# Seven block products instead of eight in the last block of three projections

## The chip, the core and the metric

The kernel runs on one core of one Trainium2 chip. The metric is device time in microseconds (us) from launch to end, as the median of several runs. One execution was also profiled: it gives the start and the length of every instruction on the engines. These are TensorE (PE; its weight loads are listed apart as PEld), VectorE (DVE), ScalarE (ACT), GpSimd (POOL) and the queue of SyncE (SP) that issues DMAs.

## The reference

The kernel computes one layer of a streaming encoder on 2048 tokens of width 1024, in float32:

```
u = rms_norm(h, g_mix_pre);  z = u @ w_in
ya = swa_with_sinks(...z...);  yh = hgrn2(...z...)          # two groups of heads
y = concatenate([ya, yh]) @ w_out                           # the out projection
h = h + rms_norm(y, g_mix_post)
u = rms_norm(h, g_x_pre);  m = rms_norm(mem, g_mem)
s = (u @ wq) . (m @ wk);  p = softmax(s);  y = (p . (m @ wv)) @ wo   # 4 heads, 256 memory tokens
h = h + rms_norm(y, g_x_post)
u = rms_norm(h, g_ffn_pre)
y = (silu(u @ w_gate) * (u @ w_up)) @ w_down
h = h + rms_norm(y, g_ffn_post)
```

The kernel folds wq with the memory's keys into one 1024 x 1024 matrix, and the memory's values with wo into another. So the cross attention is two more products of the same form: tokens by "qk" gives the scores, softmax of the scores by "vo" gives the output.

## The kernel before

A float32 factor is split into a high part that TensorE takes directly (fp32r) and the remainder, low. A product of two such factors is three matmuls: high by high, high by low, low by high (L1122, L1123 and L1124 in `products`).

**Jobs and blocks.** Behind the attention, the work is a list of jobs (`jobs`, L1418): the out projection, the scores ("qk"), the values ("vo"), two halves of the gate and up projections of the feed-forward part, and three parts of the down projection. A job holds one resident operand, called T, of 2 x 2 quarters (each up to four slices of 128 rows, 512 columns), and streams the other, called S, in blocks. The out projection, the scores and the values have eight blocks each, of 256 tokens. A block multiplies a 2 x 2 split of S with the 2 x 2 split of T.

**Two kinds of block.** A block of kind "s" (`seven`, L1126) does Winograd's form of Strassen's scheme: seven products of quarters instead of eight. It takes sums and differences of the quarters: `combine` makes four for S on DVE (L1097), and those for T are made beforehand in DRAM (`combined`). Three intermediate products are copied out of PSUM by ACT (L1137) and added by DVE when a result is taken out (L1498 for the out projection and the values, L1557 for the scores). A block of kind "p" (`eight`, `plain`) does the plain eight products: four quarters of S, no sums, and the results leave PSUM by a copy on ACT alone (L1500), or directly into the softmax. Its products come in an order of its own, and of T it needs the four plain quarters, numbered 1, 2, 8 and 3; a block of kind "s" needs 1, 5, 6, 3, 7, 2 and 4.

**Making operands.** Every S quarter is split by `split2` (L982): the high part on ACT (L985) or POOL (L987), then the low part on DVE (L988), 128 x 512 each. Every T operand comes in two halves of 128 x 1024: a DMA into a row tile, the high part on ACT, the low part on DVE, the same lines. T operands live in seven slots. A slot becomes free with the last step that uses its operand; `half` (L1262) then issues the load of one half of the next operand in order of need, and `split` issues the splitting of a half that was loaded.

**What sets the order.** `phases` (L1210) walks through the steps: after each step (one product in a block of kind "s", two in one of kind "p") it makes the S quarters of two steps ahead, gives each follow-up piece of work of earlier blocks (`after`) a turn, and calls `split` and `half`: once per step in a block of kind "s", twice in one of kind "p". These lines hold for the last block of a job if it is of kind "s" (and `fresh` for the block behind it):

```
change = kind == "s" and i == len(bl) - 1
...
if change or kind == "s" and fresh:
    split(g)
    if change and q in (0, 3, 6):
        half(g, self.row_tile)
```

So such a block splits up to two halves per step, and loads a second one in three of its seven steps. The follow-up work of a block is RMS norms, residual adds, the softmax's scaling, transposes by TensorE (L1381) and stores: L1529 and L1530 for the out projection, L1571 and L1573 for the scores, L1617, L1608 and L1604 for the values, where two blocks also prepare sums of tokens (`token_sums`, L1409 to L1413). A planner of the framework, which estimates times, then fixes the final order of the instructions on every engine; engines run their own queues in that order and wait on each other's semaphores.

In `jobs`, `kinds(blocks, n, last)` gives the first n blocks kind "p", the last block kind `last` (default "p") and the others "s". Before the change, the out projection has kind "p" in its first and its last block, and the scores and the values in their last; the feed-forward jobs have "s" throughout.

Of the kernel before, what the change touches and what calls it, by code (L numbers as in the profile page):

```python
# [29 lines left out]
NT = T // P  # L30
# [18 lines left out]
class Layer:  # L49
# [1121 lines left out]
    def plain(self, S, T, nk, out, keep, kind):  # L1171
# [36 lines left out]
        yield  # L1208

    def phases(self, jobs, first, prologue=None):  # L1210

        steps = [(n, i, p) for n, job in enumerate(jobs) for i, b in enumerate(job[2])
                 for p in self.STEPS[b[0]]]
        takes = [c for job in jobs for b in job[2] for c in self.TAKES[b[0]]]
# [200 lines left out]
    def jobs(self):  # L1418
        I = self.I

        def weights(src, r0, nk):
            return lambda t, i, j, k0, n: self.load(
                t, src[r0 + (i * nk + k0) * P:r0 + (i * nk + k0 + n) * P, j * 512:(j + 1) * 512]
                .rearrange("(k p) d -> p k d", p=P))

        def ffn_u(b):
            return lambda t, i, j, k0, n: self.load(
                t, self.u_d[4 * i + k0:4 * i + k0 + n, :, b * TB + j * 512:b * TB + (j + 1) * 512]
                .rearrange("k p t -> p k t"))

        def kinds(blocks, n=0, last="p"):
            return [("p" if i < n else last if i == len(blocks) - 1 else "s",) + b for i, b in enumerate(blocks)]

        def sums(name, src, nk, other=None):
            return self.sums(name, src, nk, self.extra_tile, other or self.gain_tile)

        def in_turn(*what):
            return lambda: itertools.chain.from_iterable(w() for w in what)

        qk, vo = weights(self.qk_d, 0, 4), weights(self.vo_d, 0, 4)  # L1440
        down = [(weights(I["w_down"], f0 * P, nk), f0, nk) for f0, nk in ((0, 3), (6, 4), (14, 4))]
        qk_s, vo_s = sums("qk_s", qk, 4, self.row_tile), sums("vo_s", vo, 4)
        u_s = sums("u_s", ffn_u(1), 4)
        self.u0_s = self.tc.dram_tile([4, P, 4 * 512], F32, name="u0_s")
        d_s = [sums(f"d_s{c}", src, nk) for c, (src, _, nk) in enumerate(down)]
        jobs = [(self.w_out, 4, kinds([self.mixed_block(n) for n in range(0, NT, 2)], 1), self.out_sums, {1: [qk_s[1]]}),
                (qk, 4, kinds([self.score_block(n) for n in range(0, NT, 2)]), qk_s[0], {1: [vo_s[1]]}),
                (vo, 4, kinds([self.value_block(n) for n in range(0, NT, 2)]), vo_s[0], {})]
        for b in range(NB):
            beside = {2: [in_turn(*(d[1] for d in d_s))]} if b else {4: [u_s[1]]}  # L1450
            jobs.append((ffn_u(b), 4, kinds([blk for f in range(0, NFF, 2) for blk in self.hidden_blocks(b, f)], 0, "s"),
                         u_s[0] if b else self.u0_s, beside))
        for c, (src, f0, nk) in enumerate(down):
            jobs.append((src, nk, kinds([self.down_block(c, f0, nk, n) for n in range(0, NT, 2)], 0, "s"), d_s[c][0], {}))

        return jobs
# [308 lines left out]
```

## Time and profile before

| | us |
|---|---|
| median of 3 runs | 2574.08 |
| lowest and highest | 2572.68, 2574.33 |
| profiled execution, its time | 2572.97 |
| profiled execution, its span from first to last instruction | 2571.3 |
| TensorE busy | 2535.4 |
| VectorE busy | 1764.8 |
| ScalarE busy | 1263.9 |
| GpSimd busy | 425.4 |

Groups of instructions are listed by line, engine, operation and tiles (written <- read), with their count, busy time and mean length in ns, then the engine's idle time before them with what ended it. In a timeline a row has start and length in us, the engine, and in brackets the engine's idle time ahead of it. A table of stretches gives for each stretch its length, the busy time of each engine with the instructions in parentheses, TensorE's granted clock, and the share of the DMA engines. The out projection, the scores and the values run from about 785 us to 1300 us of the span.

### The profile page before, as it was taken

How to read it: one execution, taken by the hardware profiler on the slowest of the kernel's cores; microseconds unless marked ns; L12 is line 12 of the kernel's file. 1: busy time of each engine (PE TensorE's matmuls, PEld its weight loads, DVE VectorE, ACT ScalarE, POOL GpSimd, SP SyncE). 2: the span in 40 equal slices, each digit the busy share in tenths (PEclk: the TensorE clock that was granted, in tenths of full speed). 3: DMA queues.
4: the chain of work that ended last, by engine and by line, in shares of the span. 5: the costliest groups of instructions: out<-in, count | busy, mean ns of one | idle time of the engine just before them, and what ended most of it. 6: DMA issues, size and time to landing. Idle time of an engine off the chain costs nothing.

```text
span 2571.3 us, 34876 instructions
## 1 busy us (share of the span) xinstructions
PE 2535.4 (99%) x12326; PEld 2124.0 (83%) x12326; DVE 1764.8 (69%) x2791; ACT 1263.9 (49%) x2643; POOL 425.4 (17%) x612
## 2 busy tenths in 40 slices
PE   9999999999999999999999999999999999999998
PEld 8888888878987888888778888888888888888886
DVE  7785588887556778788885655576666557574766
ACT  5563466555555565565563333344333335443543
POOL 4231334321312322212310000000000000000022
PEclk9999999999999999999999999999999999999999
DMA  5445755765887896665973622253555425464776
GB/s 189 148 164 170 205 162 163 228 198 160 262 282 276 294 310 209 221 218 198 341 244 117 205 91 74 82 205 117 186 197 196 156 94 182 165 195 106 226 178 152
DMA packets 357295, 486.36 MB, mean 189 GB/s; under 512 B 20352, under 2 KB 248704, under 8 KB 357120
## 3 DMA queue, kind: packets, MB, share of 16 engines
q1 hardware_dynamic: 351072, 462.11, 54.6%
q0 software_dynamic: 6048, 22.02, 4.9%
q8 instruction: 97, 1.59, 0.3%
q14 instruction: 78, 0.64, 0.1%
HBM read 317.34 MB, written 166.72 MB: 188 GB/s over the span
## 4 chain that ended last, share of the span: by engine, by line
PE 82%; DMA 6%; DVE 6%; ACT 2%; issue 2%; POOL 1%; SPq 1%; DVEq 0%; POOLq 0%; ACTq 0%
PE psm L1122 22%; PE psm L1124 22%; PE psm L1123 22%; PE psg L157 2%; PE psg L156 2%; PE psg L158 2%; PE pss L1381 1%; DMA x<-in_w_out_dram 1%; DVE S L988 1%; DMA y_d<-sg 1%; DMA u_d<-row 1%; DVE T L988 0%; SPq L75 0%; DMA qk_s<-extra 0%; DVE S L808 0%
## 5 line engine op out<-in xcount | busy, mean ns | idle before, releaser
L1123 PE MATMUL psm<-T,S 128*128 128x512 f32 x2680 | 1042.9, 390 | 1.4 <-DVE T L988 1.4
L1122 PE MATMUL psm<-T,S 128*128 128x512 f32 x2680 | 1035.2, 391 | 4.9 <-ACT part L1137 3.4
L1124 PE MATMUL psm<-T,S 128*128 128x512 f32 x2680 | 1030.5, 390 | 4.9 <-DVE S L988 4.9
L1122 PEld LDWEIGHTS psm<-T,S 128*128 128x128 f32 x2680 | 503.0, 188 | 113.3 <-ACT part L1137 6.0
L1124 PEld LDWEIGHTS psm<-T,S 128*128 128x128 f32 x2680 | 503.1, 188 | 111.4 <-DVE S L988 7.0
L1123 PEld LDWEIGHTS psm<-T,S 128*128 128x128 f32 x2680 | 503.2, 188 | 106.4 <-DVE T L988 3.8
L985 ACT ACTIVATE S<-sum 128x512 fp32r<-128x512 f32 (+1 forms) x330 | 198.6, 619 | 364.1 <-PE psm L1124 260.9
L988 DVE TENSOR_TENSOR S<-sraw,S 128x512 fp32r<-128x512 f32 (+1 forms) x315 | 214.6, 689 | 229.8 <-ACT S L985 216.4
L988 DVE TENSOR_TENSOR S<-sum,S 128x512 fp32r<-128x512 f32 (+1 forms) x388 | 259.1, 677 | 47.1 <-ACT S L985 32.6
L1137 ACT ACTIVATE part<-psm 128x512 f32<-128x512 f32 x285 | 168.9, 596 | 244.9 <-PE psm L1124 223.6
L985 ACT ACTIVATE S<-sraw 128x512 fp32r<-128x512 f32 (+1 forms) x268 | 165.2, 617 | 110.0 <-PE psm L1124 99.4
L1509 POOL DMA_DIRECT2D y_d<-row x16 | 14.0, 877 | 1077.4 <-DVE row L1695 1026.6
L988 DVE TENSOR_TENSOR T<-row,T 128x1024 fp32r<-128x1024 f32 (+1 forms) x112 | 131.8, 1189 | 35.9 <-ACT T L985 34.1
L157 PE MATMUL psg<-u,whi 128*128 128x512 f32 x320 | 127.8, 399 | 0.0
L158 PE MATMUL psg<-u,wlo 128*128 128x512 f32 x320 | 127.1, 397 | 0.0
L156 PE MATMUL psg<-u,whi 128*128 128x512 f32 x320 | 127.1, 397 | 0.0
L1476 ACT ACTIVATE junk<-row 128x512 f32<-128x512 f32 x160 | 99.7, 625 | 45.7 <-DVE row L1498 27.2
L985 ACT ACTIVATE T<-row 128x1024 fp32r<-128x1024 f32 (+1 forms) x112 | 113.6, 1032 | 8.6 <-DMA row<-d_s 4.3
L987 POOL TENSOR_SCALAR S<-sum 128x512 fp32r<-128x512 f32 x58 | 49.4, 851 | 300.1 <-PE psm L1124 240.9
L1646 DVE TENSOR_TENSOR row<-psm,part 128x512 f32<-128x512 f32 x66 | 43.7, 688 | 68.3 <-PE psm L1124 68.2
L1655 DVE TENSOR_TENSOR part<-psm,part 128x512 f32<-128x512 f32 x66 | 43.8, 688 | 60.2 <-PE psm L1124 60.0
L1695 DVE TENSOR_TENSOR row<-psm,part 128x512 f32<-128x512 f32 x72 | 49.1, 688 | 49.5 <-PE psm L1124 49.4
(364 smaller groups left out, 3715.6 us busy)
## 6 DMA issues: line engine op xcount, KB each, us to landing
sraw<-in_w_gate_dram SPq DMA_DIRECT2D x44, 512.0 KB, 3.6
sraw<-in_w_up_dram SPq DMA_DIRECT2D x44, 512.0 KB, 3.7
hid_d<-row SPq DMA_DIRECT2D x44, 512.0 KB, 2.7
sraw<-hid_d SPq DMA_DIRECT2D x32, 512.0 KB, 4.1
sraw<-in_w_in_dram SPq DMA_DIRECT2D x44, 256.0 KB, 3.6
z_d<-pair SPq DMA_DIRECT2D x20, 512.0 KB, 3.0
raw<-in_w_in_dram SPq DMA_DIRECT2D x20, 512.0 KB, 4.6
z_d<-z SPq DMA_DIRECT2D x20, 512.0 KB, 4.0
```

The costliest lines, as they stand in the source:

```text
L156: nc.tensor.matmul(ps, ah, bh, start=(i == 0), stop=False)
L157: nc.tensor.matmul(ps, ah, bl, start=False, stop=False)
L158: nc.tensor.matmul(ps, al, bh, start=False, stop=(i == n - 1))
L985: self.nc.scalar.activation(hi, raw, AF.Copy)
L987: self.nc.gpsimd.tensor_scalar(hi, raw, 1.0, 1.0, ALU.mult, ALU.mult)
L988: self.nc.vector.tensor_tensor(lo, raw, f32(hi), ALU.subtract)
L1122: nc.tensor.matmul(ps, s[:, 0, k, :], t[:, 0, k, :], start=st, stop=False, **kw)
L1123: nc.tensor.matmul(ps, s[:, 0, k, :], t[:, 1, k, :], start=False, stop=False, **kw)
L1124: nc.tensor.matmul(ps, s[:, 1, k, :], t[:, 0, k, :], start=False, stop=sp, **kw)
L1137: nc.scalar.activation(t, ps, AF.Copy)
L1476: self.nc.scalar.activation(junk, a, AF.Square, scale=float(D) ** -0.5, accum_out=to)
L1695: nc.vector.tensor_tensor(d, a, b, ALU.add)
```

## The change

The last block of the out projection, of the scores and of the values becomes a block of seven products. With that the rule on last blocks quoted above, of two splits per step, holds for these three changes of job as well, and the block behind each is `fresh`. The first block of the out projection stays one of eight products.

```diff
-        jobs = [(self.w_out, 4, kinds([self.mixed_block(n) for n in range(0, NT, 2)], 1), self.out_sums, {1: [qk_s[1]]}),
-                (qk, 4, kinds([self.score_block(n) for n in range(0, NT, 2)]), qk_s[0], {1: [vo_s[1]]}),
-                (vo, 4, kinds([self.value_block(n) for n in range(0, NT, 2)]), vo_s[0], {})]
+        jobs = [(self.w_out, 4, kinds([self.mixed_block(n) for n in range(0, NT, 2)], 1, "s"), self.out_sums, {1: [qk_s[1]]}),
+                (qk, 4, kinds([self.score_block(n) for n in range(0, NT, 2)], 0, "s"), qk_s[0], {1: [vo_s[1]]}),
+                (vo, 4, kinds([self.value_block(n) for n in range(0, NT, 2)], 0, "s"), vo_s[0], {})]
```

In the built programs, TensorE's order differs from the last block of the out projection to the third block of the feed-forward part (the other queues from about a block earlier), and is the same ahead of and behind that. TensorE has 36 matmuls fewer (12 each of L1122, L1123 and L1124). VectorE has nine more low splits of S (12 more that read a sum, 3 fewer that read a loaded quarter), twelve more sums (L1097), nine more adds on the way out of PSUM (six at L1498, three at L1557) and six fewer splits of T halves. ScalarE has nine more high splits of S, nine more copies (L1137), six copies fewer (L1500) and six high splits of T halves fewer. GpSimd has as many instructions as before. SyncE issues eight DMAs fewer: two from qk, four from w_out, two from vo.

## The prediction

> **What bounds the kernel now.** I read the page first, then TensorE's weight loads in order of time, then a table of stretches around each change of job, and then the groups and VectorE's timeline at these places.
>
> ```profile
> span 2571.3 us, 34876 instructions
> PE 2535.4 (99%) x12326; PEld 2124.0 (83%) x12326; DVE 1764.8 (69%) x2791; ACT 1263.9 (49%) x2643; POOL 425.4 (17%) x612
> PEclk9999999999999999999999999999999999999999
> PE 82%; DMA 6%; DVE 6%; ACT 2%; issue 2%; POOL 1%; SPq 1%; DVEq 0%; POOLq 0%; ACTq 0%
> ```
>
> TensorE is busy 99% of the span at the full granted clock, and carries 82% of the chain that ended last. So time goes down if TensorE has fewer matmuls, as long as nothing else makes it wait. What one matmul costs shows in two weight loads of one line, three matmuls apart, in a feed-forward block without waits:
>
> ```profile
> 1350.33 0.19 PEld L1123 LDWEIGHTS psm<-T,S 128*128 128x128 f32 x1
> ...
> 1351.01 0.19 PEld L1123 LDWEIGHTS psm<-T,S 128*128 128x128 f32 x1
> ```
>
> 0.68 us for three, 0.227 us each. A block of 84 at that spacing takes 19.0 us. The next rows have that block first, then the first block behind three changes of job where the last block is already of kind "s", and then the stretches around the three changes that are edited (the last block of eight products, and what follows it).
>
> ```profile
> core 0: us, PE busy (x) PEld busy (x) DVE busy (x) ACT busy (x) POOL busy (x), PEclk, DMA share, GB/s
> 1340.60:1359.60 19.00, 19.00 (x85) 15.74 (x84) 9.98 (x16) 7.37 (x14) 0.00 (x0) 1.00 0.45 154
> 1721.40:1741.60 20.20, 19.51 (x85) 15.58 (x84) 19.63 (x26) 11.91 (x18) 0.00 (x0) 1.00 0.47 157
> 2255.70:2275.90 20.20, 19.84 (x84) 15.27 (x83) 20.20 (x26) 15.09 (x21) 0.00 (x0) 1.00 0.76 291
> 2409.20:2428.40 19.20, 19.20 (x85) 15.61 (x84) 17.78 (x22) 13.83 (x20) 0.87 (x1) 1.00 0.81 245
> ...
> 930.00:953.00 23.00, 23.00 (x111) 19.11 (x111) 16.79 (x17) 18.10 (x39) 5.33 (x10) 1.00 0.89 317
> 953.00:975.00 22.00, 22.00 (x107) 18.08 (x106) 21.03 (x26) 16.19 (x33) 8.05 (x13) 1.00 0.88 306
> ...
> 1126.00:1148.00 22.00, 21.28 (x103) 17.58 (x102) 19.76 (x28) 15.89 (x29) 2.81 (x4) 1.00 0.48 161
> ...
> 1274.00:1296.00 22.00, 22.00 (x107) 18.37 (x106) 17.44 (x18) 20.23 (x44) 6.08 (x9) 1.00 0.87 314
> 1296.00:1318.00 22.00, 21.69 (x104) 17.77 (x103) 21.42 (x25) 16.05 (x27) 2.73 (x3) 1.00 1.04 360
> ```
>
> Two things are to be seen. At a change of job VectorE is the second bound: it is busy 19.6 to 21.4 us of 20 to 22, since fourteen halves of the next T have to be split there. And the blocks of eight products leave it slack: 16.79 of 23 us and 17.44 of 22. The three changes that already have seven products lose 1.2, 1.2 and 0.2 us in the block behind them, against 19.0. (A fourth, into the first part of the down projection, is left out: its T halves are smaller.)
>
> What the edited changes lose now stands in the waits of the weight loads:
>
> ```profile
> 967.74 0.19 PEld L1123 LDWEIGHTS psm<-T,S 128*128 128x128 f32 x1 [0.30 <-DVE T L988]
> 967.84 0.19 PEld L1124 LDWEIGHTS psm<-T,S 128*128 128x128 f32 x1
> ...
> 1128.39 0.79 PEld L1381 LDWEIGHTS pss<-ident,row 128*128 128x128 f32 x7
> 1130.14 0.19 PEld L1122 LDWEIGHTS psm<-T,S 128*128 128x128 f32 x1 [0.95 <-ACT part L1137]
> ...
> 1321.43 0.19 PEld L1123 LDWEIGHTS psm<-T,S 128*128 128x128 f32 x1 [1.07 <-DVE T L988]
> ...
> 1323.44 0.19 PEld L1122 LDWEIGHTS psm<-T,S 128*128 128x128 f32 x1 [0.18 <-ACT part L1137]
> ```
>
> There are twelve such gaps between 967 and 1324 us, outside the blocks that make token sums, 5.7 us beyond the spacing in all (0.4, 1.8 and 3.5 at the three changes). Behind a gap the next load follows after about 0.10 us instead of 0.227, so each gives back 0.11 us: the net loss is 0.15, 1.4 and 2.8, together 4.4 us.
>
> **The change part by part.** *Removed on TensorE:* 36 matmuls at 0.227 us, **8.2 us**, all on the path, as TensorE has no slack there. [...]
>
> *Added on VectorE, moved off it:* prices are start to start, from rows in which one instruction follows another.
>
> ```profile
> 1300.45 0.68 DVE L988 TENSOR_TENSOR S<-sum,S 128x512 fp32r<-128x512 f32 x1
> 1301.05 1.22 DVE L988 TENSOR_TENSOR T<-row,T 128x1024 fp32r<-128x1024 f32 x1
> 1302.18 2.48 DVE L1604 SCALAR_TENSOR_TENSOR row<-row,q_r,g 128x1024 f32<-128x1024 f32 x2
> 1304.58 0.69 DVE L1097 TENSOR_TENSOR sum<-sraw,sum 128x512 f32<-128x512 f32 x1
> ```
>
> A 128x512 operation takes 0.60 us, a T half 1.13, a step of 1024 columns of the norms 1.20. Per change VectorE gets three more splits, four more sums and three more adds, ten by 0.60, and loses two T halves (T8 isn't needed a second time): 6.0 - 2.3 = 3.7 us more, in a block that TensorE leaves 2.7 us sooner. Its slack of some 4.6 to 6.2 us in that block (above) is eaten up, and then the order decides. So I counted, in the built order, what VectorE has to do from the last result that it must wait for (an add out of PSUM, released by a product's end) to the operand half that TensorE needs next, where this is worst:
>
> - Out projection to scores: 10 T halves, 7 S splits, 5 sums, 3 adds, 2 maxima of the softmax, 4 steps of the norm (L1529, L1530): 11.3 + 10.2 + 4.8 = 26.3 us. TensorE has 103 matmuls and 28 transposes (about 0.1 us each) in between, 26.1 us. Short by 0.2; with L1530 at its own, longer record about 0.4.
> - Scores to values: 5 T halves, 5 S splits, 3 sums, 2 adds, 3 maxima, 2 small reciprocals, 4 scalings (L1573, 0.36 less the overlap of 0.08): 14.8 us against 51 matmuls and 16 transposes, 13.1 us. Short by 1.7.
> - Values to feed-forward: 9 T halves, 4 S splits, 3 sums, 1 add, 6 steps of the norms (L1617, L1604, L1608): 22.1 us against 77 matmuls and 16 transposes, 19.1 us. Short by 3.0.
>
> Together **5.1 us** that TensorE must wait if VectorE never pauses. The same count by the full records (these groups) gives the upper bound:
>
> ```profile
> L988 DVE TENSOR_TENSOR T<-row,T 128x1024 fp32r<-128x1024 f32 x105 | 127.2, 1223 | 35.9 <-ACT T L985 34.1 <-DMA row<-u_s 1.7
> L988 DVE TENSOR_TENSOR S<-sum,S 128x512 fp32r<-128x512 f32 x356 | 241.5, 688 | 38.9 <-ACT S L985 24.4 <-POOL S L987 12.0
> L1097 DVE TENSOR_TENSOR sum<-sum,sraw 128x512 f32<-128x512 f32 x89 | 62.0, 696 | 1.6
> L1498 DVE TENSOR_TENSOR row<-psm,part 128x512 f32<-128x512 f32 x39 | 26.6, 682 | 4.0 <-PE psm L1124 3.1 <-ACT part L1137 0.9
> L1617 DVE SCALAR_TENSOR_TENSOR row<-row,q_r,extra 128x1024 f32<-128x1024 f32 x16 | 20.2, 1300 | 3.7 <-DMA out_dram<-row 1.8 <-DMA row<-h_d 1.4 <-POOL q_r L1491 0.6
> L1573 DVE TENSOR_SCALAR row<-row,mc 128x256 f32<-128x256 f32 x64 | 19.3, 364 | 0.2
> ...
> L1561 DVE TENSOR_REDUCE x_mx<-row 128x2 f32<-128x512 f32 x21 | 14.2, 678 | 0.1
> ```
>
> That is 29.3, 16.8 and 24.3 us, short by 3.2, 3.7 and 5.2, **12.1 us**. Records overlap their successors by 0.08 us in the timeline, so I take the lower count. It leaves out VectorE's waits: for ACT's high halves (34.1 us over 105 T halves) and for DMAs. By the same count no change of the kernel before is short, yet they lost 0.15, 1.4, 2.8, 1.2, 1.2 and 0.2 us: 1.2 on average, which I add at each change, 3.6 us.
>
> *Behind the waiting instruction* on VectorE stand the S splits two steps ahead and the adds that free PSUM; TensorE waits for the first, for the second only when its six banks are full.
>
> *ScalarE* gets nine high splits, nine copies, and loses six copies and six T halves: about 1 us over three changes. It is busy 16 to 20 of 22 us with overlapping records, so I price it at nothing; if that cover is gone, its lateness is part of the 3.6. *GpSimd's* count is the same. *SyncE* issues eight loads fewer and is moved past nothing that was late; T halves can now be requested only as slots come free, one per product, but the one needed first has seven products, 19 us, for load and split.
>
> *Sum:* -8.2 + (5.1 + 3.6) - 4.4 = **-3.9 us** on the profiled execution, 2572.97 to 2569.1. The median stands 1.1 us above that execution, so **2570.2 us**. A measurement of this kernel can tell 0.2% or 5.1 us from no change, and the forecast lies inside that. Bounds: without pauses of VectorE -7.5, by the full records +3.3.
>
> **The rivals.**
>
> *A. The work is hidden (faster by more than 5.1).* What VectorE could not do in time was also moved: the planner lets TensorE take products of the next block first, and the waits at ACT that now cost 4.4 us need not come back. For it: the third change with seven products loses only 0.2 us with VectorE busy 17.78 of 19.2. Against it: VectorE at 21.42 of 22.00 already without the added 3.7. It gives -7.5, up to -8.2 if the waits come to what they are now: 2565.9 to 2566.6.
>
> *B. VectorE pauses more than at other changes.* Then the count by full records is nearer, and the time 2573 to 2577. For it: follow-up work waits for DMAs in VectorE's queue, as here, and everything behind it stands:
>
> ```profile
> 1294.57 1.28 DVE L1617 SCALAR_TENSOR_TENSOR row<-row,q_r,extra 128x1024 f32<-128x1024 f32 x1 [1.75 <-DMA out_dram<-row]
> ...
> 899.04 1.67 POOL L987 TENSOR_SCALAR S<-sum 128x512 fp32r<-128x512 f32 x1 [3.67 <-PE psm L1124]
> 908.14 0.62 POOL L987 TENSOR_SCALAR S<-sum 128x512 fp32r<-128x512 f32 x1 [7.44 <-DVE S L988]
> ```
>
> With slack such a pause costs nothing; without, all of it. Against it: the three feed-forward changes lost at most 1.2.
>
> *C. GpSimd's splits become late (slower).* One high split of S took 0.62 us in one place and 1.67 in another, while VectorE was packed with operations on two tiles. VectorE will be packed for longer, three splits per block are GpSimd's, and the two blocks at three changes have 18. If TensorE waits for the 1.05 us in n of them, the time rises by 1.05 n beyond the forecast: slower than before from n = 4, by over 0.2% from n = 9, 2579 us and more. Against it: S is made two steps, 5.4 us, ahead. [...]
>
> That the change doesn't do what it says is excluded by the counts of the built program.
>
> **How the numbers follow.** The forecast, a gain of 2 to 5.1 us, 0.42; rival A 0.30; rival B, from a gain of 2 to a loss of 5.1, 0.15; rival C 0.13. So faster by over 0.2%: 0.30; within: 0.57; slower: 0.13. The range from 2566.3 to 2577.5 takes in both bounds of the sum and leaves out about 0.1 at either end; the forecast's own range is 2568.9 to 2572.
>
> **What would show it.** TensorE's matmuls of L1122 to L1124 fall by 12 each. VectorE is busy over 19 us of 20.6 in each new last block, and there are gaps of about 1.5, 3 and 4 us at the three changes, named by T or S of L988. The feed-forward part behind its third block is unchanged. No gaps beyond 4.4 us means A; gaps released by ACT or DMA ahead of L988, over 10 us, mean B; L987 at 1 us and more ahead of a waiting L988 means C. The forecast is wrong altogether if the gaps lie elsewhere, such as in loads issued late.

## The result and the profile after

The changed kernel takes 2585.76 us (median of 6 runs, 2583.78 to 2590.15). Beside it the kernel before takes 2573.53 us (6 runs, 2570.75 to 2574.80). The ratio is 1.0047, with a 95% interval from 1.0033 to 1.0060: slower by about 12 us, where the prediction had 4 us less than before and a range that ended at 2577.5. The profiled execution took 2583.78 us, the lowest of its runs; that of before took 2572.97, near its median.

First the head of the profile's page of the changed kernel, then a table of stretches: the new last block of the out projection, and the block behind the change at each of the three changes.

```profile
span 2582.1 us, 34812 instructions
PE 2534.7 (98%) x12290; PEld 2121.4 (82%) x12290; DVE 1772.9 (69%) x2815; ACT 1262.5 (49%) x2649; POOL 440.2 (17%) x612
```

```profile
core 0: us, PE busy (x) PEld busy (x) DVE busy (x) ACT busy (x) POOL busy (x), PEclk, DMA share, GB/s
930.00:950.60 20.60, 20.46 (x100) 16.65 (x98) 17.04 (x21) 14.82 (x30) 5.81 (x8) 1.00 0.92 327
950.60:969.60 19.00, 13.96 (x58) 10.83 (x58) 16.91 (x18) 11.93 (x21) 10.33 (x9) 0.91 0.95 346
...
1126.00:1147.00 21.00, 17.21 (x73) 13.16 (x72) 16.79 (x28) 14.88 (x28) 5.78 (x3) 0.92 0.74 262
...
1307.00:1326.00 19.00, 14.10 (x64) 11.65 (x63) 17.94 (x19) 14.13 (x26) 4.96 (x6) 0.91 1.06 372
```

TensorE has the 36 matmuls less (12326 to 12290) but is busy as long as before, 2534.7 against 2535.4 us. Two new things stand in the table: behind each change TensorE stands idle for 4 to 5 us of about 20, and its granted clock is 0.91 or 0.92 there, where the table of before had 1.00 in every row.

Five waits of TensorE at and ahead of the three changes, from its timeline (the bracket is the idle time ahead of the row and what ended it). Two more of 1.29 and 1.20 us, for ScalarE, stand at 1127.93 and 1159.81. The kernel before waits 1.50 us, too, where the one at 1264.26 stands.

```profile
956.46 0.50 PE L1122 MATMUL psm<-T,S 128*128 128x512 f32 x1 [3.61 <-ACT part L1137]
968.21 0.50 PE L1122 MATMUL psm<-T,S 128*128 128x512 f32 x1 [1.22 <-POOL S L987]
...
1140.52 0.50 PE L1122 MATMUL psm<-T,S 128*128 128x512 f32 x1 [2.13 <-POOL S L987]
...
1264.26 0.62 PE L1124 MATMUL psm<-T,S 128*128 128x512 f32 x1 [2.38 <-DVE S L988]
...
1312.31 0.45 PE L1381 MATMUL pss<-ident,row 128*128 128x128 f32 x1 [4.90 <-DVE row L1617]
```

To compare kernels I add up, at each change, by how much each weight load starts later than its spacing (0.227 us behind a matmul, 0.10 behind a transpose; only delays over 0.07 us), and apart from it the excess of the matmuls that run at half clock (explained below). The stretches are 915 to 1000, 1100 to 1200 and 1225 to 1345 us, token sums included, so the sum of before, 13.6 us, is above the 5.7 us that the prediction counted outside them.

| waits + half clock, us | out to scores | scores to values | values to feed-forward | sum |
|---|---|---|---|---|
| before | 1.8 + 0 | 3.6 + 0 | 8.2 + 0 | 13.6 + 0 |
| after | 9.4 + 1.4 | 10.4 + 1.6 | 12.1 + 1.8 | 31.9 + 4.8 |

This carries the loss: 18.3 us more of waits and 4.8 us of half clock, against 8.2 us of matmuls saved. That is 14.9 us. The spans differ by 10.8 only, as the profiled execution of the changed kernel was already 4.1 us ahead at 830 us (the same weight load starts at 825.69 instead of 829.77), where both kernels have the same order; that is scatter between two executions, and part of it is one wait of 1.7 instead of 2.7 us.

By the brackets over 0.3 us between 915 and 1345 us, ScalarE ended 6.5 us of TensorE's idle time in the changed kernel against 0.7 before, GpSimd 3.4 against 0, and VectorE 8.4 against 3.6, of which L1617 is 4.9.

### The profile page after: what moved, and what is told of

Same layout as the page of the kernel before. It is cut to its first block, busy times and chain, and to the rows that moved or that the text cites. A ratio compares the mean times of both kernels' runs of the same rounds, so it can differ in the third digit from the quotient of the medians.

```text
span 2582.1 us, 34812 instructions
## 1 busy us (share of the span) xinstructions
PE 2534.7 (98%) x12290; PEld 2121.4 (82%) x12290; DVE 1772.9 (69%) x2815; ACT 1262.5 (49%) x2649; POOL 440.2 (17%) x612
## 4 chain that ended last, share of the span: by engine, by line
PE 52%; DMA 1%; DVE 1%; ACT 1%; issue 1%; POOL 0%; SPq 0%; DVEq 0%; POOLq 0%; ACTq 0%
PE psm L1124 17%; PE psm L1122 17%; PE psm L1123 17%; DMA row<-in_w_down_dram 1%; PE pss L1381 1%; ACT junk L1476 0%; DMA u_d<-row 0%; ACT T L985 0%; DVE S L988 0%; DVE T L988 0%; DVE row L1608 0%; SPq L75 0%; DVE row L1713 0%; ACT S L985 0%; ACT part L1137 0%
## 5 line engine op out<-in xcount | busy, mean ns | idle before, releaser
L1122 PE MATMUL psm<-T,S 128*128 128x512 f32 x2668 | 1034.0, 392 | 14.5 <-ACT part L1137 7.6
L1123 PE MATMUL psm<-T,S 128*128 128x512 f32 x2668 | 1040.2, 391 | 0.6 <-DVE T L988 0.6
L1124 PE MATMUL psm<-T,S 128*128 128x512 f32 x2668 | 1029.0, 391 | 4.4 <-DVE S L988 4.4
L1122 PEld LDWEIGHTS psm<-T,S 128*128 128x128 f32 x2668 | 502.0, 188 | 124.3 <-ACT part L1137 12.1
L1124 PEld LDWEIGHTS psm<-T,S 128*128 128x128 f32 x2668 | 502.3, 188 | 111.7 <-DVE S L988 7.5
L1123 PEld LDWEIGHTS psm<-T,S 128*128 128x128 f32 x2668 | 502.5, 188 | 105.6 <-DVE T L988 2.8
L988 DVE TENSOR_TENSOR S<-sraw,S 128x512 fp32r<-128x512 f32 (+1 forms) x312 | 210.8, 684 | 229.4 <-ACT S L985 213.2
L988 DVE TENSOR_TENSOR S<-sum,S 128x512 fp32r<-128x512 f32 (+1 forms) x400 | 267.7, 678 | 43.6 <-ACT S L985 28.3
L1137 ACT ACTIVATE part<-psm 128x512 f32<-128x512 f32 x294 | 173.8, 596 | 248.9 <-PE psm L1124 228.3
L988 DVE TENSOR_TENSOR T<-row,T 128x1024 fp32r<-128x1024 f32 (+1 forms) x106 | 124.8, 1192 | 30.7 <-ACT T L985 28.8
L987 POOL TENSOR_SCALAR S<-sum 128x512 fp32r<-128x512 f32 x64 | 66.2, 1034 | 337.0 <-PE psm L1124 258.2
L985 ACT ACTIVATE T<-row 128x1024 fp32r<-128x1024 f32 (+1 forms) x106 | 107.7, 1030 | 10.5 <-DMA row<-d_s 5.1
```

The source lines that it names most:

```text
L985: self.nc.scalar.activation(hi, raw, AF.Copy)
L987: self.nc.gpsimd.tensor_scalar(hi, raw, 1.0, 1.0, ALU.mult, ALU.mult)
L988: self.nc.vector.tensor_tensor(lo, raw, f32(hi), ALU.subtract)
L1122: nc.tensor.matmul(ps, s[:, 0, k, :], t[:, 0, k, :], start=st, stop=False, **kw)
L1123: nc.tensor.matmul(ps, s[:, 0, k, :], t[:, 1, k, :], start=False, stop=False, **kw)
L1124: nc.tensor.matmul(ps, s[:, 1, k, :], t[:, 0, k, :], start=False, stop=sp, **kw)
```

## Three causes in the profile

**Copies out of PSUM stand last in ScalarE's full queue.** Busy time in the same three stretches, first of the kernel before, then of the changed one (columns as in the table above):

```profile
943.20:956.50 13.30, 13.30 (x64) 11.08 (x64) 12.28 (x15) 11.90 (x26) 5.31 (x9) 1.00 0.84 280
1121.60:1136.60 15.00, 14.28 (x76) 11.90 (x75) 13.22 (x24) 11.85 (x23) 3.25 (x5) 1.00 0.43 154
1298.00:1312.30 14.30, 13.99 (x71) 11.42 (x69) 14.30 (x17) 10.62 (x17) 2.33 (x3) 1.00 1.02 350
```

```profile
943.20:956.50 13.30, 9.47 (x47) 7.35 (x45) 11.39 (x15) 13.27 (x29) 8.06 (x9) 1.00 0.96 347
1121.60:1136.60 15.00, 13.34 (x61) 10.28 (x60) 15.00 (x26) 15.00 (x29) 4.29 (x4) 1.00 0.91 324
1298.00:1312.30 14.30, 9.41 (x42) 7.49 (x41) 12.96 (x18) 12.99 (x28) 3.35 (x5) 1.00 1.01 338
```

ScalarE goes from 11.90 to 13.27 of 13.30 us, from 11.85 to 15.00 of 15.00, and from 10.62 to 12.99 of 14.30. Its share of the whole span did not change (49%). But these are stretches of equal time, not of equal work, and a full ScalarE alone stops nothing. Two rows of the kernel before, the first only 2 us later, have it as full, while TensorE is busy throughout:

```profile
945.20:958.50 13.30, 13.30 (x68) 11.15 (x67) 12.28 (x15) 13.29 (x27) 5.34 (x9) 1.00 0.95 314
1288.30:1302.60 14.30, 14.30 (x73) 12.01 (x72) 12.54 (x15) 14.30 (x28) 5.14 (x6) 1.00 1.02 352
```

What differs is what stands in the queue. A last block of eight products has no copy of L1137; one of seven has three, and TensorE can need the bank that such a copy frees (3.61 us of waiting at 956.46). The timeline of ScalarE in the changed kernel, ahead of the wait at 956.46:

```profile
951.34 1.06 ACT L985 ACTIVATE T<-row 128x1024 fp32r<-128x1024 f32 x1
952.29 0.58 ACT L1500 ACTIVATE row<-psm 128x512 f32<-128x512 f32 x1
952.77 0.62 ACT L985 ACTIVATE S<-sraw 128x512 fp32r<-128x512 f32 x1
953.29 1.08 ACT L1382 ACTIVATE row<-pss 128x512 f32<-128x512 f32 x2
954.24 0.64 ACT L1476 ACTIVATE junk<-row 128x512 f32<-128x512 f32 x1
...
954.85 1.07 ACT L985 ACTIVATE T<-row 128x1024 fp32r<-128x1024 f32 x1
955.80 0.60 ACT L1137 ACTIVATE part<-psm 128x512 f32<-128x512 f32 x1
```

The copy of L1137, on which TensorE waits for its PSUM bank, is last in a queue without gaps: two T halves of 1.06 us, an S quarter, copies of transposes, a square for the norm. TensorE stopped at 952.85 (956.46 less 3.61). The wait at 1312.31 goes back to ScalarE in part: the transposes wait for VectorE's L1617, this for a reciprocal root on GpSimd, and that for a square on ScalarE. Rows of GpSimd, then of VectorE:

```profile
1308.63 0.62 POOL L1487 TENSOR_TENSOR q_v<-q_s 128x2 f32<-128x2 f32 x1 [18.88 <-ACT junk L1476]
...
1309.64 1.21 POOL L1491 TENSOR_TENSOR q_r<-q_w,mhalf 128x2 f32<-128x2 f32 x1
```

```profile
1310.88 2.48 DVE L1617 SCALAR_TENSOR_TENSOR row<-row,q_r,extra 128x1024 f32<-128x1024 f32 x2 [0.60 <-POOL q_r L1491]
```

VectorE stood idle 0.60 us for this root, and 0.25 and 0.39 us for ScalarE's high parts in the 7 us before. So some 1.2 us of the 4.90 are lateness of the other two in this execution; the rest is VectorE's own queue, in which L1617 stands behind splits and sums.

**A few splits on GpSimd become very long.** The view of one source line sums up L987 between 770 and 1350 us (durations in ns, shortest, median, longest), first before, then after:

```profile
L987 POOL TENSOR_SCALAR S<-sum x40: 617/716/1730, 792.7 to 1249.3; 128x512 fp32r<-128x512 f32 x40
L987 POOL TENSOR_SCALAR S<-sraw x29: 615/990/1848, 806.3 to 1269.6; 128x512 fp32r<-128x512 f32 x29
```

```profile
L987 POOL TENSOR_SCALAR S<-sum x46: 618/826/4241, 789.6 to 1281.3; 128x512 fp32r<-128x512 f32 x46
L987 POOL TENSOR_SCALAR S<-sraw x23: 613/698/1655, 803.2 to 1286.7; 128x512 fp32r<-128x512 f32 x23
```

Of 69 splits before, none took over 1.85 us; of 69 after, the longest took 4.24 and another 3.47, and these two end the waits at 968.21 and 1140.52. In both kernels the time of a split goes with VectorE: where VectorE ran no operation with two SBUF inputs in the split's first 0.6 us, it took 0.61 or 0.62 us (25 splits before, 27 after); the others took 0.62 to 1.85 us before and 0.62 to 4.24 after. Here are the two long ones, with VectorE's queue at the first:

```profile
963.91 4.24 POOL L987 TENSOR_SCALAR S<-sum 128x512 fp32r<-128x512 f32 x1 [6.17 <-PE psm L1124]
...
1137.00 3.47 POOL L987 TENSOR_SCALAR S<-sum 128x512 fp32r<-128x512 f32 x1 [6.54 <-PE psm L1124]
```

```profile
963.59 1.22 DVE L1530 TENSOR_TENSOR row<-row,row 128x1024 f32<-128x1024 f32 x1
964.72 2.36 DVE L988 TENSOR_TENSOR T<-row,T 128x1024 fp32r<-128x1024 f32 x2
966.99 0.69 DVE L988 TENSOR_TENSOR S<-sraw,S 128x512 fp32r<-128x512 f32 x1
967.60 0.69 DVE L1557 TENSOR_TENSOR row<-psm,part 128x512 f32<-128x512 f32 x1
```

The split starts beside a VectorE operation that reads two SBUF tiles, lasts through three more of them without a pause between, and ends at 968.15, 0.55 us after VectorE begins L1557, which takes one operand from PSUM. The split of 3.47 us ends in the same way, at 1140.47, 0.56 us after VectorE begins L1498 (which reads psm and part) at 1139.91. What holds GpSimd back in the meantime, the rows do not show.

**TensorE runs at half clock behind a long wait.** Weight loads from its timeline, behind the wait at 956.46:

```profile
956.57 0.19 PEld L1123 LDWEIGHTS psm<-T,S 128*128 128x128 f32 x1
956.80 0.19 PEld L1124 LDWEIGHTS psm<-T,S 128*128 128x128 f32 x1
...
958.08 0.33 PEld L1122 LDWEIGHTS psm<-T,S 128*128 128x128 f32 x1
958.50 0.33 PEld L1123 LDWEIGHTS psm<-T,S 128*128 128x128 f32 x1
...
960.90 0.19 PEld L1123 LDWEIGHTS psm<-T,S 128*128 128x128 f32 x1
961.14 0.19 PEld L1124 LDWEIGHTS psm<-T,S 128*128 128x128 f32 x1
```

After some 0.8 us at the usual spacing of 0.23 us, the spacing is 0.42 to 0.43 for 3.4 us, and then 0.23 again. By the view of stretches the granted clock is 0.50 from 957.29 to 960.70 us and 1.00 in the 7.28 us ahead of it and the 5.29 us behind it. The four such stretches of this execution cost 1.4, 1.6 and, the last two together, 1.8 us more than their matmuls should: the 4.8 us of the table. The first three follow the waits at 956.46, 1140.52 and 1264.26, the fourth the one at 1312.31. The prediction took the clock as full throughout.

## The experiments

Ratios are to the kernel before on the same chip, with 95% intervals; its medians there were 2573.42 (first four kernels), 2570.86 (e5 to e8), 2573.23 (e9 to e12), 2572.08 (e13 to e15) and 2575.61 us (e16, e17).

**One change of job at a time.** `"s"` for the last block in only one of the three jobs, for instance the scores, against the kernel before:

```diff
-                (qk, 4, kinds([self.score_block(n) for n in range(0, NT, 2)]), qk_s[0], {1: [vo_s[1]]}),
+                (qk, 4, kinds([self.score_block(n) for n in range(0, NT, 2)], 0, "s"), qk_s[0], {1: [vo_s[1]]}),
```

> The out projection alone ends in a block of seven products; scores and values keep theirs of eight. By the gaps between the weight loads of the full change, the change from out projection to scores got 9.0 us more of waiting for 2.7 us of matmuls saved: 4 to 6 us slower than before if the three changes are independent. If only one of the three did the harm, or they add up through the clock, it is within 1 us of before. Theory 1 (GpSimd's high splits of S stretched beside a packed VectorE): the splits at this change still take over 2 us each. Theory 2 (ScalarE's queue late): gaps ended by copies of L1137 here too. Theory 3 (VectorE's count alone): no gap over 1 us here, as the count is short by 0.4 only, and the time 2 us below before.

> The scores alone end in a block of seven products. By the gaps, 8.9 us more waiting for 2.7 us saved: 4 to 6 us slower than before if independent. Theory 1: a GpSimd split of over 3 us right ahead of the longest gap. Theory 3 (VectorE's count, short by 1.7): 1 us faster than before.

> The values alone end in a block of seven products. By the gaps, 4.8 us more waiting for 2.7 us saved, 1 to 3 us slower than before; the longest gap, some 5 us, again ahead of transposes that wait for L1617. The three single changes should add up to the 12 us of the whole within 3 us; a sum far below would mean that they need each other. Theory 3 (short by 3.0): within 1 us of before.

The out projection alone takes 2579.75 us, 1.0028 [1.0017, 1.0039]; the scores alone 2582.69, 1.0035 [1.0021, 1.0049]; the values alone 2580.99, 1.0028 [1.0017, 1.0040]. Each is slower by 6 to 9 us, though each removes only 12 matmuls, and the three do not add up to the whole. Waits and half clock at the edited change alone are 10.2 + 1.4, 10.4 + 1.6 and 10.7 + 1.4 us. Less what the kernel before has there and the 2.7 us of matmuls, this is a loss of 7.1, 5.7 and 1.2 us, where the whole change loses 6.3, 5.7 and 3.0; so the first two changes of job lose by themselves, and the third hardly does. The sum of the times fails because the planner reacts elsewhere too: in all three the order in the down projection differs from that of before, and a wait of some 3 us for L1137 stands near 2420 us, which the whole change does not have. The values alone lose also at the first change, which they leave as it was:

In that kernel the out projection's change has the queues' order of before. Even so one split there, which took 1.13 us before, took this:

```profile
962.60 5.80 POOL L987 TENSOR_SCALAR S<-sum 128x512 fp32r<-128x512 f32 x1 [5.56 <-PE psm L1124]
```

It started 0.5 us behind VectorE's L1530 at 962.10 and ended 0.55 us behind the start of L1557 at 967.85. TensorE waited 2.80 us for it at 968.46, and ran at half clock behind. So whether such a split is short or long depends on its start against VectorE's queue, not on the order alone.

**GpSimd's splits to ScalarE.** The splits of the last block of a job and of the first block behind the change are forced to ScalarE. Those of the second block behind it, which are made two steps ahead, stay on GpSimd:

```diff
-            t, src[n:n + 2, :, 512 * j:512 * j + 512].rearrange("i p c -> p i c")), 4, kind, tiles=True)
+            t, src[n:n + 2, :, 512 * j:512 * j + 512].rearrange("i p c -> p i c")), 4, kind,
+            "A" if n == NT - 2 or n == 0 and src is not self.y_d else None, tiles=True)
```

> The changed kernel, but in the last block of out projection, scores and values and the first block of scores and values all high splits of S are ScalarE's, none GpSimd's. Theory 1: the gaps that end with a GpSimd split of S (2.4 us and 1.6 us, with the halved clock behind the first another 1.6 us) are gone, 4 to 7 us faster than the changed kernel, so 5 to 9 us slower than before turns into that. Theory 2: ScalarE gets 15 splits of 0.53 us more where it is packed, and the gaps behind its copies and squares grow: 0 to 5 us slower than the changed kernel. Theory 3: no change, as VectorE has the same work.

2583.93 us, 1.0043 [1.0029, 1.0057]: no gain that can be told. At the first change the wait for the copy out of PSUM grows from 3.61 to 5.13 us; at the second the wait for GpSimd stays. The long split there (2.88 us at 1137.9) is one of the second block, so this run did not take the late split away. Rows of TensorE:

```profile
959.11 0.79 PE L1122 MATMUL psm<-T,S 128*128 128x512 f32 x1 [5.13 <-ACT part L1137]
...
1140.79 0.50 PE L1122 MATMUL psm<-T,S 128*128 128x512 f32 x1 [2.17 <-POOL S L987]
```

**ScalarE's squares left out.** The second norm's statistics of the last two blocks are not computed (its scale is taken from the first norm's), without and with the edit of e4:

```diff
-                self.mean_squares(y[i], i, s2)
+                if n < NT - 4:
+                    self.mean_squares(y[i], i, s2)
...
-            r = self.rstds(s2)
+            r = self.rstds(s2 if n < NT - 4 else ss[0])
```

> The changed kernel without the second pair of mean squares (L1476, four per block of 256 tokens, 0.7 us each on ScalarE) of the last two blocks of the out projection and of the values; the norm uses the first mean squares in their place, so this part of the computation is left out. Theory S (ScalarE's queue has no slack at a change of seven products, and what stands behind the squares is late): the long waits at 952.5 (3.9 us, ended by a copy L1137 behind squares) and 1306.8 (5.2 us, transposes behind L1617 behind squares) go, and with them the some 2.4 us of matmuls at half clock behind them: 10 to 11 us less than the changed kernel, 2574 to 2576 us. Theory V (VectorE's queue is short, as predicted, or GpSimd's splits wait for VectorE): ScalarE's squares do not matter, the waits get another name, 2583 to 2586 us.

> The same without squares (that part is left out), and in addition the high splits of S that GpSimd made in the last block of the three jobs and in the first block of the scores and the values are made by ScalarE, nine and six in all. Theory S with GpSimd as the second cause: the waits that end with GpSimd at 966.4 and 1261 (1.6 and 2.8 us, and the half clock behind the latter, 1.6) go as well, as ScalarE now has room for the splits: 2569 to 2573 us. If GpSimd's waits cost nothing of their own: the same as without squares alone, within 2 us. If ScalarE is still without slack: slower than without squares alone by 2 us and more.

2587.78 us, 1.0064 [1.0051, 1.0077], and 2582.67 us, 1.0045 [1.0032, 1.0058]. Taken alone this would speak against ScalarE. But in e5 another cause takes the place: VectorE's queue shifts, and a split on GpSimd takes 5.19 us, with TensorE waiting 3.78 us for it at 972.63. In e6, where again only the second block's splits are left on GpSimd, one takes 5.80 us, and TensorE waits 2.62 us for it at 972.77 and 1.48 for another at 1144.95. The wait for L1617 is gone in both; some 2.7 us of waits for ScalarE's copies are left in its place. The long split of e5:

```profile
967.39 5.19 POOL L987 TENSOR_SCALAR S<-sum 128x512 fp32r<-128x512 f32 x1 [3.81 <-PE psm L1124]
```

**The follow-up work later.** In the last two blocks the second norm and what follows wait 6 or 12 turns longer, and read the rows again from DRAM; the same on the kernel before:

```diff
+            if n >= NT - 4:
+                for _ in range(12 if n == NT - 4 else 6):
+                    yield
+                for i in range(2):
+                    y[i] = self.rows_of(self.h1_d, n + i)
```

> The changed kernel, all of the computation: the second half of the follow-up work (squares, norm, transposes) of the last two blocks of the out projection and of the values waits twelve and six turns, until behind the change of job, and loads its rows again from DRAM. Theory S: the squares and the copies of transposes no longer stand in ScalarE's queue at these two changes, 9 to 11 us less than the changed kernel, 2574 to 2577 us. Theory V: nothing is gained, as VectorE has as much to split: 2583 to 2587 us; a gain of 3 to 5 us would be VectorE's, as the norms' steps (L1617, 4 of 1.2 us) move too at the values' change, and then the out projection's change shows none.

> The kernel before with the same deferral of follow-up work. Under theory S the blocks of eight products leave ScalarE room, so there is little to gain: the waits between 967 and 1324 us are 5.7 us gross, of which ScalarE ends about 3: 2571 to 2574 us. Then the changed kernel with the deferral should stand at most 4 us above this one, instead of 12. If the deferral itself were worth 8 us and more here too, it would say nothing on the change.

2587.27 us, 1.0063 [1.0047, 1.0079], and 2573.57 us, 1.0005 [0.9993, 1.0016]. On the kernel before it changes nothing; on the changed one it does not help. Waits and half clock are 10.5 + 1.4, 10.0 + 1.6 and 12.0 + 3.6 us: the longest at the first change is now for a split on GpSimd (3.96 us). The work that was moved is late behind the changes instead: at 1326.95, for instance, TensorE waits 1.67 us for a T half's high part on ScalarE.

**Only the splits of the second block behind the change to ScalarE** (three each in the scores and the values, the two long ones among them), alone and on the kernel before, and together with the edit of e5; then also without VectorE's residual adds (L1530, L1608) and softmax scalings (L1573) in the last two blocks:

```diff
+            "A" if n == 2 and src is not self.y_d else None, tiles=True)
```

```diff
+                if n < NT - 4:
+                    nc.vector.tensor_tensor(y[i], y[i], x[i], ALU.add)
...
-                for h in range(4):
+                for h in range(4 if n < NT - 4 else 0):
```

> The changed kernel with the three high splits of S that GpSimd made in the second block of the scores and in the second block of the values (six in all) made by ScalarE. One of them took 4.24 us at 963.9 and one 3.47 us at 1137.0, and TensorE waited 1.6 and 2.4 us for them, with 1.4 us of half clock behind the second; in the two kernels with the squares left out or deferred the first cost 4.1 and 4.3 us. Theory P (GpSimd's split cannot run while VectorE works without pause on two operands in SBUF, and TensorE waits for it): these waits go, 4 to 6 us less than the changed kernel, 2580 to 2582 us. Rival V (VectorE is late at these places anyway, GpSimd only stands in front): the waits stay under VectorE's name, 2584 to 2587 us.

> The kernel before with the same six splits on ScalarE. By theory P the kernel before loses to them only in some executions (one split of 5.80 us cost 3.1 us and half clock behind it in an execution with the order of the kernel before; in the profiled one it was 1.13 us and cost nothing): 0 to 2 us faster, 2569 to 2572 us, and less spread. If ScalarE has no room for six splits: 1 to 3 us slower.

> The changed kernel without the second mean squares of the last two blocks of the out projection and of the values (that part is left out), and with the six splits on ScalarE. If ScalarE and GpSimd are two causes that stand in for each other, the sum shows here: the waits of 4.05 and 2.38 us for GpSimd in the kernel with only the squares left out go, and about 2.8 us of half clock: 2576 to 2580 us. If it is VectorE's packed queue behind both, 2584 to 2587 us.

> The same, and in addition VectorE's residual adds (L1530, L1608) and the scalings of the softmax (L1573) of the last two blocks of the three jobs are left out, 4.8, 4.8 and 4.5 us of VectorE's time at the three changes. If VectorE's queue is short at these changes, as the prediction counted (5.1 to 12.1 us), this takes most of what is left of the waits: 2564 to 2570 us, below the kernel before. If VectorE was never the one that is late: within 2 us of the kernel without squares and with the six splits moved.

| | median us | ratio | waits + half clock at the changes |
|---|---|---|---|
| e9, splits | 2582.70 | 1.0039 [1.0025, 1.0054] | 7.6 + 1.4, 7.6 + 0, 12.8 + 1.6 |
| e10, on before | 2573.13 | 1.0002 [0.9993, 1.0012] | |
| e11, splits and squares | 2578.56 | 1.0016 [1.0004, 1.0028] | 6.0 + 0, 8.0 + 0, 11.1 + 1.2 |
| e12, also VectorE's work | 2576.11 | 1.0014 [1.0001, 1.0026] | 5.1 + 1.2, 7.0 + 0, 8.9 + 1.4 |

The two reliefs that failed singly work together: 1.0016 against 1.0047. Each had been covered by the other's wait, as the rows of e5 above show for the squares; in e9 the wait for the copy (3.63 us) and the one for L1617 (4.90) stay. Taking some 14 us of work from VectorE as well adds nothing that can be told.

**VectorE's work alone**, left out of the changed kernel without the other two edits:

> The changed kernel with only VectorE's residual adds (L1530, L1608) and the softmax's scalings (L1573) of the last two blocks of the three jobs left out: 4.8, 4.8 and 4.5 us of VectorE's time at the three changes, ScalarE's work as it is. If VectorE's short queue, the 5.1 us of the prediction, were the loss: 5 us and more less than the changed kernel, below 2581 us. If ScalarE is what is late: 2583 to 2587 us. A gain of 2 to 4 us could also be GpSimd's, whose splits then find pauses of VectorE: its rows tell.

2580.99 us, 1.0035 [1.0022, 1.0048], some 3 us better than the whole change, within the intervals. Not all of that is VectorE's own: the split that had taken 4.24 us takes 0.62 here, while TensorE still waits 2.73 us for the copy out of PSUM. The wait for L1617 shrinks from 4.90 to 3.77 us.

```profile
967.19 0.62 POOL L987 TENSOR_SCALAR S<-sum 128x512 fp32r<-128x512 f32 x1 [8.31 <-PE psm L1124]
```

**All statistics left out.** With the splits of e9, both norms of the last two blocks of the out projection and of the values use the scale of an earlier block, and no squares are computed; the same two edits on the kernel before:

```diff
-            r = self.rstds(ss[0])
+            r = self.rstds(ss[0]) if n < NT - 4 else self.r_x[:, 0:2]
```

> The changed kernel with the six splits of S on ScalarE, and without any mean squares (first and second, L1476, with GpSimd's steps behind them) in the last two blocks of the out projection and of the values; a factor of an earlier block stands in for them, so this part of the computation is left out. ScalarE gets rid of eight more squares of 0.7 us per change beside the kernel with only the second ones left out and the splits moved. If ScalarE's queue is still the late one there (copies L1137 at 952 and 1302, 1.6 us each, copies of transposes 1.6 us): 3 to 5 us less than that kernel, 2573 to 2576 us. If what is left has another cause: within 2 us of it, 2577 to 2580 us.

> The kernel before with the same part left out as in the changed kernel without statistics (no mean squares in the last two blocks of the out projection and of the values), and with the six splits on ScalarE. If ScalarE's full queue is particular to the change of seven products, the kernel before gains little, 0 to 3 us (it waits for ScalarE about 3 us gross at these places): 2570 to 2573 us, and with ScalarE relieved the change is worth some 3 to 6 us, near the 8.2 us of its matmuls less what is left of the waits. If leaving the statistics out is worth 5 us and more here too, the 17 us between the changed kernel and the one without statistics are in good part not the change's.

2567.21 us, 0.9984 [0.9975, 0.9993], and 2571.02 us, 0.9978 [0.9967, 0.9989]. The quotient says what the change is worth where ScalarE is relieved on both sides: 0.9984 / 0.9978 = 1.0006, with an interval of about 0.0014 to either side from those of the two (squares added, root). So the loss of 0.47% goes to none that can be told; a gain of the 8.2 us of the matmuls (0.32%) does not appear either. The table of stretches of e13 shows it:

```profile
943.20:956.50 13.30, 13.30 (x71) 11.12 (x70) 12.79 (x15) 10.03 (x15) 5.50 (x2) 1.00 1.03 387
...
1121.60:1136.60 15.00, 14.62 (x72) 11.74 (x72) 14.75 (x24) 12.72 (x25) 0.72 (x1) 1.00 0.78 288
1298.00:1312.30 14.30, 13.78 (x69) 11.31 (x68) 14.30 (x18) 10.60 (x17) 0.00 (x0) 1.00 1.03 351
```

ScalarE is at 10.03, 12.72 and 10.60 us, TensorE has 71 matmuls instead of 47 in the first stretch and no half clock in any, and VectorE is nearly full, 12.79, 14.75 and 14.30 us, without harm in the first. Waits and half clock are 2.2, 7.8 and 9.6 + 0.6 us (e17: 1.9, 3.9 and 4.4). What stays at the second change is still ScalarE, in copies out of PSUM and splits behind the softmax; at the third it is one wait of 4.6 us at 1250 for a split on VectorE, which had stood 2.85 us for a DMA (u_d<-row), in a block that makes token sums. The edit takes away both ScalarE's squares and the chain through GpSimd's reciprocal roots, and with them the order of the queues changes; how much each of these carries was not tried apart.

**The clock by itself.** On the kernel before, one low split in ordinary feed-forward blocks is written again and again, so that TensorE has to wait there for VectorE; a small and a large number of repetitions:

```diff
+        for _ in range(again):
+            nc.vector.tensor_tensor(m[:, 1], t, f32(m[:, 0]), ALU.subtract)
```

> The kernel before with waits made on purpose where TensorE otherwise has none: in the second half of the gate and up projections nine times the low split of one S operand is done again 9, 10, ... 17 times by VectorE (0.6 us each) before TensorE may use it; it was made some 5.4 us ahead, so the waits should be 1 to 5 us. If the half clock follows from idle time in a fixed window of 3.41 us: none behind waits under 2.1 us, some behind 2.2 to 4.5 us (by where the window's border falls), all behind longer ones, each stretch ending on one grid of 3.41 us and costing up to 1.7 us beyond the wait. If it has to do with the changes of job (loads, power) and not with the wait: no matmul at 0.43 us here.

> As the first probe, in which the order by the planner left only one wait (2.48 us), but with 20, 22, ... 36 repetitions instead of 9 to 17, 12 to 22 us of VectorE's time, so that TensorE must wait several times, some waits far above 3.41 us. If the half clock follows from idle time in a fixed window of 3.41 us: every wait over 4.5 us is followed by matmuls 0.43 us apart, waits under 2.1 us by none, and all such stretches end on one grid of 3.41 us. If it belongs to the changes of job and not to the wait: none here.

2573.87 and 2602.27 us, one run each. The small number was hidden: 117 more operations, some 70 us of VectorE's work, left the time within the scatter of the kernel before, and made one wait of 2.5 us without half clock. The large one made waits of several lengths. Weight loads around two of them:

```profile
2069.08 0.19 PEld L1128 LDWEIGHTS psm<-T,S 128*128 128x128 f32 x1 [2.01 <-DVE S L988]
2069.19 0.19 PEld L1126 LDWEIGHTS psm<-T,S 128*128 128x128 f32 x1
2069.42 0.19 PEld L1127 LDWEIGHTS psm<-T,S 128*128 128x128 f32 x1
...
2083.59 0.29 PEld L1128 LDWEIGHTS psm<-T,S 128*128 128x128 f32 x1 [4.21 <-DVE S L1112]
...
2084.19 0.33 PEld L1127 LDWEIGHTS psm<-T,S 128*128 128x128 f32 x1
2084.62 0.33 PEld L1128 LDWEIGHTS psm<-T,S 128*128 128x128 f32 x1
```

Behind 2.01 us the spacing is 0.23 at once; behind 4.21 us it is 0.43. The granted clock of this run is 0.52 from 2083.60 to 2088.80 us, behind the longer of the two. So half clock followed a long wait here, with no change of job near.

No kernel that does all of the work beat the kernel before; e8 and e10, which do not have the change, equal it.

## Why the prediction was wrong

- *Removed on TensorE, 8.2 us:* right. The counts fell by 36 and the spacing is still 0.227 us.
- *VectorE's queue short by 0.4, 1.7 and 3.0 us:* about right in size in all, but not by the steps counted, and not what decided. TensorE's idle time that VectorE ended grew by 4.8 us (3.6 to 8.4), near the 8.7 less 4.4 us of the sum. But 4.9 us of it is the one wait for L1617, not for T or S of L988, and some 1.2 us of that are lateness of ScalarE and GpSimd. Leaving out 14 us of VectorE's work bought about 3 us alone and nothing that can be told on top of the other reliefs, and e13 runs its first change almost without a wait with VectorE busy 12.79 of 13.30 us. The new last block of the out projection, predicted with VectorE busy over 19 us of 20.6, has 17.04.
- *"ScalarE ... I price it at nothing":* this is the step that failed. It set one more microsecond over three changes against a mean of 16 to 20 of 22 us. In place of nothing, the waits that ScalarE ended grew from 0.7 to 6.5 us; the cover, "part of the 3.6", was reached by the one wait at 956.46 alone. Added busy time was the wrong measure: ScalarE was full there before, too (13.29 of 13.30 us from 945.2), at no cost to TensorE. The change put copies out of PSUM behind T halves, copies of transposes and squares, in a queue whose rows follow one another without a gap from 951.34 to 956.40.
- *Today's waits of 4.4 us subtracted:* wrong. The waits at these places came back longer and did not go.
- *GpSimd, "count is the same", and rival C:* the count was right and said nothing. C named the late splits, and this rival came true in part, but not by its price: not 1.05 us in many of 18 splits, but 2.9 to 3.6 us beyond the normal 0.62 in two, for which TensorE waited 3.4 us instead of nothing. Moving six splits away brought about 2 us (1.0047 to 1.0039, within the intervals); together with the squares left out, 1.0016. C alone did not reach the measured time.
- *The clock:* not thought of. The prediction read the full granted clock of the kernel before as given; 4.8 us of the loss came from it, a cost that followed waits of 2.13 to 4.90 us here and made them dearer.
- *The upper bound:* by its own terms, -8.2 + 12.1 + 3.6 - 4.4, it is +3.1 us and not +3.3; this changes nothing in the account.
- *The feed-forward part behind its third block unchanged:* right. *Gaps over 10 us, released by ACT or DMA ahead of L988:* the gaps came to over 10 us, but the longest that ScalarE released stand ahead of matmuls, for a copy (L1137), and not ahead of VectorE's splits. B's mechanism, VectorE pausing for DMAs, was not at work: between 915 and 1345 us VectorE waited 3.7 us for DMAs, and 11.6 in the kernel before.

By the experiments, about 10 of the 12 us hang on ScalarE and GpSimd together (1.0047 against 1.0006 for the change with both relieved; by the two intervals this is 10 us, give or take 5), the half clock being part of what these waits cost. How they share it cannot be told singly, as each covers the other. Why the 8.2 us of the matmuls do not show even then is open: waits stay at the second and third change, and none of the runs removed them.

## What to carry to other kernels

An engine with half of the span busy (ScalarE, 49%) can have none of its time free in the 13 us that count (13.27 of 13.30), and even that does not say whether it will be waited for (13.29 of 13.30 in the kernel before, without a wait). Read its busy time in stretches as short as the one in which the added work must be done, and then ask what stands in its queue ahead of the one copy that frees TensorE's PSUM bank. When several engines are late at the same place, relieving one may show nothing (1.0064 in e5 and 1.0039 in e9, beside 1.0047; 1.0016 for both together in e11); take away two together, and do the same to the kernel before. Check first that an edit moves the very instructions that were late, which e4 and e6 did not. A wait on TensorE can cost more than its length: here the one of 3.61 us was followed by 1.4 us of half clock, the one of 2.13 us by 1.6.

## What the runs showed of the hardware

**Half clock.** In the trace of the changed kernel the granted clock is 0.50 in four stretches of 3.41 us each, which begin at 957.29, 1141.61, 1264.49 and 1312.27 us. The beginnings are 184.32, 122.88 and 47.79 us apart, 54, 36 and 14 times 3.413. In the 3.41 us directly ahead of each, TensorE is busy 0.82, 1.28, 1.03 and 0.00 us, so at least 2.13 us are idle. With the trace cut from the same border into stretches of this length, no other one between 5 and 2571 us has more than 1.63 us idle (629.61 to 633.02). The length of a wait alone does not tell: by the brackets, one of 1.85 us (e12, at 827.85) is followed by matmuls 0.42 to 0.43 us apart, one of 2.59 us (e5, at 1270.87) and one of 2.65 us (e1, at 2426.37) are not. What sets the clock, no run shows beyond this.

**Scatter.** Over 17 runs of the kernel before, the ten with a mean clock of 0.999 have a mean time of 2570.4 us, the three with 0.997 have 2577.0. The one long wait of the kernel before, near 828 us, is an example: by the brackets 2.30 us at 829.77 without half clock in its profile, and in e12, at the same place (827.85), 1.85 us with seven spacings of 0.42 or 0.43 us behind it. So part of what varies between runs of one kernel goes with the clock, and a change that makes waits also makes such stretches more frequent: the changed kernel's clock is 0.9962 on average, that of before 0.9983.
